# Attention scores: the low half of the rotary queries in 64-row matmuls, two chunks of keys at a time

## The chip, the core and the metric

The kernel runs on one core of a Trainium2 chip. The metric is the device time of one execution in microseconds, and the kernel before is known by the median of three runs. The engines are TensorE (PE; its weight loads have a row of their own, PEld), VectorE (DVE), ScalarE (ACT), GpSimd (POOL) and the DMA queue that SyncE (SP) issues.

## What is computed

One layer of a hybrid block: a projection of 2048 latent tokens and 256 context tokens (width 1024) feeds latent attention with 4 heads and a pooling branch, and both go through one output projection. The change touches the scores of the attention alone:

```python
q = concat([q_nope, rope(q_rope)])          # 4 heads, 128 + 64
k = concat([k_nope, rope(k_rope)])          # rotary keys shared by the heads, scaled per head
s = einsum('bhqd,bhkd->bhqk', qblk, k_all) * (128 + 64) ** -0.5
p = softmax(s)                              # over 256 context keys and 2048 latent keys
o = einsum('bhqk,bhkd->bhqd', p, v_all)
```

## The kernel before

All products are made from halves, since one 16-bit number is not exact enough: each operand is a high f16 number and a low one (the remainder), written by `split()` (L99 and L100: ScalarE copies the high part, VectorE subtracts it). A product is then a sum of three: high by high, high by low, low by high.

In the first 500 us or so the kernel projects the tokens. `tok()` makes the keys of 128 tokens at a time (tile j, 18 in all). The rotary part of a key has only 64 numbers, so its high and its low half lie side by side in `krp` and are transposed together (L554): in the key tile `kd[..., 2, ...]`, partitions 0 to 63 hold the high half and 64 to 127 the low one. The rotary queries are loaded twice, to partitions 0 to 63 and to 64 to 127 (`load_q`). One matmul over 128 rows thus gives q times (high + low).

Attention goes over 16 blocks of 512 queries (4 heads by 4), each in two halves p and two blocks of 128 queries i: `scores(p, i)` is called 64 times, and "a block" below is one such call. It goes over five chunks of keys, CHUNKS, four of 512 and one of 256. For each chunk five matmuls of 128 rows are accumulated in one PSUM bank (L775): three for the 128 plain dimensions, then the high rotary queries by both halves of the keys, then the low rotary queries by both. The banks of the four big chunks come from pool A with 5 buffers, that of the last from pool X. After each chunk VectorE takes the row maximum (L778). After the last come the maximum over the chunks (L783) and its scaling (L784); ScalarE then takes the exponentials of the five banks (L796), which frees the banks, and VectorE transposes them by squares (L799). The DMA queue carries these squares across partitions (`shuffle`, L814).

Some 28 steps of scores behind, `pv()` multiplies with the values: ScalarE and GpSimd (now and then VectorE) split the probabilities (L857, L861), and TensorE runs 54 matmuls of 256 columns for each half p (L824), in a bank of pool O or X. `norm()` transposes row sums of 4 columns on TensorE (L884), and `finish()` makes three more products for each 512 queries (L916). `attn()` interleaves the two by its yields: after each chunk of scores, as many steps of `pv()` as are due. The order of each engine's instructions is then fixed at compile time by a list scheduler that estimates durations.

The startup has small matmuls that the prediction uses: L302 (weights of 2 columns), L308 (a stationary tile of 2 rows), L311 and L330 (128 rows, one moving column), L247 (448 columns).

Of the kernel before, what the change touches and what calls it, by code (L numbers as in the profile page):

```python
# [13 lines left out]
AX = mybir.AxisListType  # L14
# [15 lines left out]
KW = 1536  # L30
# [31 lines left out]
CHUNKS = ((0, 512), (512, 512), (1024, 512), (1536, 512), (2048, 256))  # L62
# [4 lines left out]
def tile_hybrid_block(ctx: ExitStack, tc: tile.TileContext, x, c, cx, c_ctx, w_mod, b_mod, norm_g,  # L67
                      w_in, q_lora_g, w_uq, kv_lora_g, w_ukv, q_norm_g, k_norm_g, w_pool,
                      pool_scale, w_out, rope_t, edge_t, out):
    nc = tc.nc  # L70
# [3 lines left out]
    q_norm_g, k_norm_g, pool_scale, c = q_norm_g[0], k_norm_g[0], pool_scale[0], c[0]  # L74
# [13 lines left out]
    def st(tag, shape, dt=F32):  # L88
        return sb.tile([128] + list(shape), dt, tag=tag, bufs=BUFS[tag], name=nm(tag))

    def pt(tag, shape=(512,), dt=F32):
        return ps.tile([128, *shape], dt, tag=tag, bufs=PBUFS[tag], name=nm("p" + tag))

    def small(n, tag):
        return sm.tile([128, n], F32, tag=tag, name=nm(tag))

    def split(src, hi, lo, eng=None):

        a = nc.scalar.activation(out=hi, in_=src, func=AF.Copy)  # L99
        (eng or nc.vector).tensor_tensor(out=lo, in0=src, in1=hi if hi.dtype == F16 else hi.bitcast(F32),  # L100
                                         op=ALU.subtract)
        return a.ins
# [290 lines left out]
    for i, g in ((0, q_norm_g), (1, k_norm_g)):  # L393
        nc.sync.dma_start(out=gr[:, i, 0], in_=g[DN:].partition_broadcast(128))
        a, b = (gr[:, i, j].rearrange("p (a b c) -> p a b c", a=2, b=2) for j in range(2))
# [43 lines left out]
    def tok(hf, k):  # L439
        is_c = hf == "c"  # L440
        c0 = QR if is_c else 0
        j = k if is_c else 2 + hf * 2 + k
# [3 lines left out]
        p = tokp.pop((hf, k), None)  # L446
        if p is None:
            p = pt("A")
# [52 lines left out]
        krs = st("U", [H, DR])  # L501
        krp = st("U", [H, 2, DR], F16)
        for h in range(H):
# [3 lines left out]
        nc.vector.tensor_tensor(out=kn, in0=k4, in1=rk.unsqueeze(2).broadcast_to([128, H, 128]), op=ALU.mult)  # L507
        nc.vector.tensor_tensor(out=krs, in0=kr.unsqueeze(1).broadcast_to([128, H, DR]),
                                in1=rk.unsqueeze(2).broadcast_to([128, H, DR]), op=ALU.mult)
        split(krs, krp[:, :, 0], krp[:, :, 1])  # L510
        ksl = slice(j * 128, (j + 1) * 128)
        if not is_c:

# [3 lines left out]
            for b in range(2):  # L517
                qp = pt("A")
                n = 0
                for i in range(2):  # L520
                    for a, w in ((lh, 0), (lh, 1), (ll, 0)):
                        nc.tensor.matmul(qp[:, 0:384], lhsT=a[:, i, :], rhs=uq[w][:, i, b * 384:(b + 1) * 384],  # L522
                                         start=(n == 0), stop=(n == 5))
# [10 lines left out]
            for a in range(2):  # L534
                for b in range(2):
                    o = a * 32 + b * 16
# [154 lines left out]
    for key, s0 in zip(TOK_ORDER, TOK_STEPS):  # L691
        g = tok(*key)
        if key in tokp:
            next(g)
        for d in AT:
            plan.setdefault(s0 + d, []).insert(0, g)
# [51 lines left out]
    def flat(t):  # L748
        return t.rearrange("p a b c d -> p (a b c d)")

    def ksegs(c0, w):
        segs = []
        while w:
            i, o = divmod(c0, KW)
            n = min(w, KW - o)
            segs.append((i, o, n))
            c0, w = c0 + n, w - n
        return segs

    def scores(p, i):  # L760

        blk = blocks[p // 2]
        kt, q = K[blk[0]], qop[blk]
        if i == 0:
            if p < 2:
                tbuf.append(st("W", [4, 2, NJ, 32]))
            TP[p] = tbuf[p % 2]
        mx = small(8, "mx")
        sp = []
        for n, (c0, w) in enumerate(CHUNKS):  # L770
            b = pt("A" if n < 4 else "X")
            s0 = 0
            for ki, o, sn in ksegs(c0, w):
                for m, (a, c, kc) in enumerate(((0, 0, 0), (0, 0, 1), (0, 1, 0), (1, 0, 2), (1, 1, 2))):
                    nc.tensor.matmul(b[:, s0:s0 + sn], lhsT=q[:, a, c, p % 2, i], rhs=kt[ki][:, kc, o:o + sn],  # L775
                                     start=(m == 0), stop=(m == 4))
                s0 += sn
            nc.vector.reduce_max(mx[:, n:n + 1], b[:, :w], axis=AX.X)  # L778
            sp.append(b)
            if n < 4:  # L780
                yield
        ng = small(1, "nm")
        nc.vector.reduce_max(ng, mx[:, 0:5], axis=AX.X)  # L783
        nc.vector.tensor_scalar(out=ng, in0=ng, scalar1=nescale, scalar2=PG * LN2, op0=ALU.mult, op1=ALU.add)  # L784
        rs = small(5, f"rs{p % 2}{i}")
        if p == NP - 1:

            for n, (c0, w) in enumerate(CHUNKS):
                nc.scalar.activation(out=flat(TP[p])[:, i * NKEY + c0:i * NKEY + c0 + w], in_=sp[n][:, :w], func=AF.Exp,
                                     bias=ng, scale=escale, accum_out=rs[:, n:n + 1])  # L790
            RS.setdefault(p // 2, []).append(rs)
            yield
            return
        for n, (c0, w) in enumerate(CHUNKS):
            e = st("T", [512])
            nc.scalar.activation(out=e[:, :w], in_=sp[n][:, :w], func=AF.Exp, bias=ng, scale=escale,  # L796
                                 accum_out=rs[:, n:n + 1])
            j0, j1 = c0 // 128, (c0 + w) // 128
            nc.vector.transpose(TP[p][:, :, i, j0:j1, :].rearrange("p q j b -> p j q b"),  # L799
                                e[:, :w].rearrange("p (j q b) -> p j q b", q=4, b=32))  # L800
        RS.setdefault(p // 2, []).append(rs)
        yield
# [192 lines left out]
    def attn():  # L995

        done = 0
        for p in range(NP):
            if p % 2 == 0 and p // 2 + 1 < len(blocks):
                load_q(blocks[p // 2 + 1])  # L1000
            gc = p * PER
            h = p // 8 + 1
            for i in range(2):
                for _ in scores(p, i):
                    gc += 1
                    lag = LAG - max(0, min(LAG - LAG_LAST, (gc - LAG_END * PER) / 4))
                    while done < (gc - lag) * 9 / PER:
                        next(pg)
                        done += 1
                    yield  # L1010
            if p == NP - 1:
                return
            with tc.issue_after(shuffle(p)):
                if h < H and p % 8 in K_PF:
                    load_k(h, (K_PF.index(p % 8),))
                if p in WO_PF:
                    load_wo(*WO_PF[p])
                if p == 30:
                    pairs.append(load_pair(0))
# [216 lines left out]
```

## Time and profile before

| | us |
|---|---|
| median of three runs | 1248.5 (1246.05 to 1248.69) |
| the profiled execution | 1248.26 |
| its span, first to last instruction | 1246.5 |
| score matmuls (L775), first to last start | 513.3 to 1054.7 |

The profile is of one execution. Busy times of TensorE are modelled from the start of a matmul to the end of its tail, so consecutive matmuls overlap in it: the time from one start to the next (the pitch) is what a matmul costs. Matmul lines of the timeline merge runs of equal instructions: the start of the first, the time to the end of the last, and their count. "128\*128 128x512" is a stationary tile of 128 rows and 128 columns, and a moving one of 512 columns.

### The profile page before, as it was taken

The page shows a single profiled execution, that of the slowest core. Times are in us where ns is not written, and L with a number is a line of the kernel's source. Part 1 is how long each engine was busy: PE and PEld are TensorE (multiplying, and loading weights), DVE is VectorE, ACT ScalarE, POOL GpSimd, SP SyncE. Part 2 cuts the span into 40 slices and gives each one's busy share as a digit, 9 for nine tenths or more (in the row PEclk, how much of TensorE's full clock was granted, in tenths as well). Part 3 has the DMA queues.
Part 4 walks back from the last instruction along what each step waited for, and adds up shares of the span by engine and source line. Part 5 has one row for each costly group of instructions (what it writes and reads, how often), then busy time and mean ns, then how long its engine had stood idle before and what let it go on. Part 6 is the DMA issues. An engine that isn't in the chain of part 4 may idle for free.

```text
span 1246.5 us, 22420 instructions
## 1 busy us (share of the span) xinstructions
PE 1186.4 (95%) x7709; PEld 936.6 (75%) x7709; DVE 914.2 (73%) x1706; ACT 761.6 (61%) x1840; POOL 602.7 (48%) x666
## 2 busy tenths in 40 slices
PE   7799999989999999889999999999999999799998
PEld 3598989989899999765666666666666666688886
DVE  4976655666556646469888788878887786999886
ACT  5585655636666655357777777777777777643221
POOL 3745313523435424014655656565565666236666
PEclk9799999999999999999999999999999999999999
DMA  9546851486326746746987797878877798515532
GB/s 304 157 130 143 212 148 45 117 201 195 86 51 149 170 91 157 197 94 151 231 198 193 169 228 192 193 187 196 227 192 191 185 244 208 181 65 206 187 130 98
DMA packets 211272, 208.67 MB, mean 167 GB/s; under 512 B 92452, under 2 KB 168533, under 8 KB 211031
## 3 DMA queue, kind: packets, MB, share of 16 engines
q1 hardware_dynamic: 211158, 207.25, 63.7%
q8 instruction: 60, 0.98, 0.3%
q14 instruction: 54, 0.43, 0.1%
HBM read 98.50 MB, written 35.56 MB: 108 GB/s over the span
## 4 chain that ended last, share of the span: by engine, by line
PE 79%; DMA 7%; ACT 5%; DVE 5%; SPq 2%; issue 2%; POOL 1%; DVEq 0%; ACTq 0%; POOLq 0%
PE pA L775 20%; PE pA L591 18%; PE pA L1049 12%; PE pA L247 6%; PE pO L824 5%; PE pX L824 5%; PE pA L522 3%; PE pX L775 2%; ACT T L796 2%; DMA M<-in_w_in_dram 2%; ACT M L857 2%; SPq L814 2%; PE pA L497 1%; DMA qrd<-U 1%; DMA B<-in_w_mod_dram 1%
## 5 line engine op out<-in xcount | busy, mean ns | idle before, releaser
L861 POOL TENSOR_TENSOR M<-W,M 128x512 f16<-128x512 f32 x244 | 277.5, 1158 | 249.1 <-ACT M L857 219.0
L775 PE MATMUL pA<-B,M 128*128 128x512 f16 x1280 | 299.5, 379 | 17.0 <-ACT T L796 14.1
L591 PE MATMUL pA<-W,B 128*128 128x256 f32 x2304 | 307.4, 287 | 0.1
L591 PEld LDWEIGHTS pA<-W,B 128*128 128x128 f32 x2304 | 290.2, 192 | 3.5 <-issue 0.9
L775 PEld LDWEIGHTS <-M 128*128 128x128 f16 x1600 | 155.6, 98 | 158.8 <-issue 20.1
L799 DVE STREAM_TRANSPOSE W<-T 128x512 f32<-128x512 f32 x310 | 193.2, 641 | 72.9 <-ACT T L796 65.8
L857 ACT ACTIVATE M<-W 128x512 f16<-128x512 f32 x279 | 164.6, 634 | 110.8 <-PE pX L824 42.4
L824 PEld LDWEIGHTS <-B 128*128 128x128 f16 x1728 | 167.7, 98 | 52.7 <-issue 16.6
L796 ACT ACTIVATE T<-pA,nm,gm 128x512 f32<-128x512 f32 x248 | 188.8, 770 | 13.6 <-DVE nm L784 13.5
L778 DVE TENSOR_REDUCE mx<-pA 128x1 f32<-128x512 f32 x256 | 169.3, 672 | 11.2 <-PE pA L775 10.6
L1049 PE MATMUL pA<-W,M 128*128 128x512 f32 (+1 forms) x528 | 120.9, 388 | 2.3 <-DVE M L1055 2.3
L824 PE MATMUL pO<-M,B 128*128 128x256 f16 x864 | 112.8, 273 | 3.8 <-POOL M L861 1.9
L824 PE MATMUL pX<-M,B 128*128 128x256 f16 x864 | 111.1, 273 | 5.3 <-DVE M L861 2.7
L1049 PEld LDWEIGHTS pA<-W,M 128*128 128x128 f32 x528 | 98.6, 190 | 22.8 <-DVE M L1055 2.7
L247 PE MATMUL pA<-B,W 128*128 128x448 f32 (+1 forms) x288 | 85.8, 369 | 0.0
L100 DVE TENSOR_TENSOR B<-M,B 128x1024 fp32r<-128x1024 f32 x48 | 61.6, 1285 | 33.0 <-ACT B L99 32.8
L99 ACT ACTIVATE B<-M 128x1024 fp32r<-128x1024 f32 (+2 forms) x53 | 55.2, 1043 | 45.7 <-DMA M<-in_w_in_dram 38.2
L1041 POOL TENSOR_TENSOR B<-T,B 128x512 f32<-128x512 f32 x31 | 50.2, 1621 | 29.5 <-DVE T L1076 27.6
L1041 POOL TENSOR_TENSOR T<-T,M 128x512 f32<-128x512 f32 x27 | 43.0, 1593 | 38.4 <-DVE T L1090 27.8
L247 PEld LDWEIGHTS pA<-B,W 128*128 128x128 f32 x288 | 54.3, 195 | 4.3 <-DVE T L278 0.9
L247 PE MATMUL pA<-W,W 128*128 128x448 f32 (+1 forms) x144 | 52.7, 367 | 0.0
L1054 ACT ACTIVATE M<-B 128x512 fp32r<-128x512 f32 x32 | 19.7, 628 | 51.6 <-PE pA L1049 39.1
(215 smaller groups left out, 1749.3 us busy)
## 6 DMA issues: line engine op xcount, KB each, us to landing
W<-W SPq DMA_DIRECT2D x496, 144.0 KB
M<-in_w_in_dram SPq DMA_DIRECT2D x48, 512.0 KB
B<-in_x_dram SPq DMA_DIRECT2D x16, 512.0 KB
B<-brd SPq DMA_DIRECT2D x8, 1024.0 KB
B<-in_x_dram SPq DMA_DIRECT2D x8, 1024.0 KB
out_dram<-B SPq DMA_DIRECT2D x31, 256.0 KB
brd<-T SPq DMA_DIRECT2D x24, 256.0 KB
kd<-T SPq DMA_DIRECT2D x36, 128.0 KB
```

The source lines that it names most:

```text
L100: (eng or nc.vector).tensor_tensor(out=lo, in0=src, in1=hi if hi.dtype == F16 else hi.bitcast(F32), op=ALU.subtract)
L247: nc.tensor.matmul(p[:, c0:NTOK], lhsT=a[:, kt, k * 128:(k + 1) * 128], rhs=b, start=(kt == 0 and n == 0), stop=(kt == KT - 1 and n == 2))
L591: nc.tensor.matmul(p[:, i * HB:(i + 1) * HB], lhsT=w[:, a, kt, :], rhs=b[:, kt, :], start=(m == 0), stop=(m == 23))
L775: nc.tensor.matmul(b[:, s0:s0 + sn], lhsT=q[:, a, c, p % 2, i], rhs=kt[ki][:, kc, o:o + sn], start=(m == 0), stop=(m == 4))
L778: nc.vector.reduce_max(mx[:, n:n + 1], b[:, :w], axis=AX.X)
L796: nc.scalar.activation(out=e[:, :w], in_=sp[n][:, :w], func=AF.Exp, bias=ng, scale=escale, accum_out=rs[:, n:n + 1])
L799: nc.vector.transpose(TP[p][:, :, i, j0:j1, :].rearrange("p q j b -> p j q b"), e[:, :w].rearrange("p (j q b) -> p j q b", q=4, b=32))
L824: i = nc.tensor.matmul(o, lhsT=V[0][:, j, a], rhs=t[:, c, jj], start=(j == 0 and m == 0), stop=(j == NJ - 1 and m == 2))
L857: a = nc.scalar.activation(out=t[:, 0], in_=s2, func=AF.Copy)
L861: lo = eng.tensor_tensor(out=t[:, 1], in0=s2, in1=t[:, 0], op=ALU.subtract)
L1041: eng.tensor_tensor(out=o[:, c0:c1] if op == ALU.mult else xr[:, k, n, c0:c1], in0=o[:, c0:c1], in1=a[:, c0:c1], op=op)
L1049: nc.tensor.matmul(b[:, c0:c1], lhsT=c[:, x0, kt, :], rhs=w[x1][:, kt, c0:c1], start=(first and kt == kts[0] and m == 0), stop=(last_ and ...
```

## The change

In `scores()` the first four matmuls of the big chunks stay as they are. The fifth, the low rotary queries, leaves out low by low: it multiplies with the high half of the keys alone, so it has 64 rows. It is put off until two chunks have had their four, and then two such matmuls follow one another, one for each chunk: that of the even chunk on partitions 0 to 63, that of the odd chunk on 64 to 127, each into the bank of its chunk. For this, `tok()` stores the rotary keys of odd chunks the other way round, low above high. The row maxima of two chunks follow the pair. The chunk of 256 keeps its five matmuls of 128 rows.

```diff
-        split(krs, krp[:, :, 0], krp[:, :, 1])
+
+        c = j // 4 % 2
+        split(krs, krp[:, :, c], krp[:, :, 1 - c])
...
-    def ksegs(c0, w):
...
         for n, (c0, w) in enumerate(CHUNKS):
             b = pt("A" if n < 4 else "X")
-            s0 = 0
-            for ki, o, sn in ksegs(c0, w):
-                for m, (a, c, kc) in enumerate(((0, 0, 0), (0, 0, 1), (0, 1, 0), (1, 0, 2), (1, 1, 2))):
-                    nc.tensor.matmul(b[:, s0:s0 + sn], lhsT=q[:, a, c, p % 2, i], rhs=kt[ki][:, kc, o:o + sn],
-                                     start=(m == 0), stop=(m == 4))
-                s0 += sn
-            nc.vector.reduce_max(mx[:, n:n + 1], b[:, :w], axis=AX.X)
             sp.append(b)
+            ki, o = divmod(c0, KW)
+            for m, (a, c, kc) in enumerate(((0, 0, 0), (0, 0, 1), (0, 1, 0), (1, 0, 2), (1, 1, 2))[:5 if n == 4 else 4]):
+                nc.tensor.matmul(b[:, 0:w], lhsT=q[:, a, c, p % 2, i], rhs=kt[ki][:, kc, o:o + w],
+                                 start=(m == 0), stop=(m == 4))
+            if n in (1, 3):
+
+                for d in (0, 1):
+                    ki, o = divmod(CHUNKS[n - 1 + d][0], KW)
+                    r = slice(64 * d, 64 * d + 64)
+                    nc.tensor.matmul(sp[n - 1 + d], lhsT=q[r, 1, 1, p % 2, i], rhs=kt[ki][r, 2, o:o + w],
+                                     start=False, stop=True)
+            for d in {1: (0, 1), 3: (2, 3), 4: (4,)}.get(n, ()):
+                nc.vector.reduce_max(mx[:, d:d + 1], sp[d][:, :CHUNKS[d][1]], axis=AX.X)
             if n < 4:
                 yield
```

## Rows read from the trace of the kernel before

**Rows 1.** The page: engines' busy time, and the chain that ended last.

```profile
PE 1186.4 (95%) x7709; PEld 936.6 (75%) x7709; DVE 914.2 (73%) x1706; ACT 761.6 (61%) x1840; POOL 602.7 (48%) x666
...
PE 79%; DMA 7%; ACT 5%; DVE 5%; SPq 2%; issue 2%; POOL 1%; DVEq 0%; ACTq 0%; POOLq 0%
```

**Rows 2.** Windows: engines' busy time in us, clock, DMA; the startup's row TensorE alone.

```profile
27.86:30.36 2.50, 2.48 (x17) 1.00 1.10 356
...
617.00:681.00 64.00, 62.58 (x413) 40.39 (x411) 52.36 (x113) 47.75 (x112) 39.16 (x34) 1.00 0.80 195
...
sum 320.00, PE 312.92 PEld 201.20 DVE 263.74 ACT 241.28 POOL 189.01; mean PE 62.58 PEld 40.24 DVE 52.75 ACT 48.26 POOL 37.80
```

**Rows 3.** Groups by line, TensorE, 640.81 to 773.45 us: count | busy us, mean ns.

```profile
L775 PE MATMUL pA<-B,M 128*128 128x512 f16 x321 | 75.3, 379 | 2.8 <-ACT T L796 2.8
L824 PE MATMUL pO<-M,B 128*128 128x256 f16 x217 | 28.5, 273 | 0.0
L824 PE MATMUL pX<-M,B 128*128 128x256 f16 x216 | 28.0, 273 | 0.0
L775 PE MATMUL pX<-B,M 128*128 128x256 f16 x80 | 11.3, 273 | 0.0
```

**Rows 4.** Timeline of TensorE in attention: start us, us to the last end, instruction, count.

```profile
807.04 3.40 PE L775 MATMUL pA<-B,M 128*128 128x512 f16 x15
810.28 0.71 PE L775 MATMUL pX<-B,M 128*128 128x256 f16 x5
810.82 0.38 PE L824 MATMUL pX<-M,B 128*128 128x256 f16 x2
811.04 0.27 PE L884 MATMUL pO<-ident,s 128*4 128x128 f32 x1
811.15 1.04 PE L824 MATMUL pX<-M,B 128*128 128x256 f16 x8
```

**Rows 5.** Timeline of TensorE, startup: tiles of 2 and 128 rows by turns.

```profile
28.24 0.38 PE L311 MATMUL pX<-ones,T 128*128 128x1 f32 x2
28.55 0.38 PE L308 MATMUL pX<-ident,T 2*128 2x2 f32 x2
...
30.10 0.38 PE L311 MATMUL pX<-ones,T 128*128 128x1 f32 x2
```

**Rows 6.** Timeline of TensorE, startup: runs of one shape.

```profile
18.61 1.05 PE L308 MATMUL pX<-ident,T 2*128 2x2 f32 x8
...
91.34 0.95 PE L330 MATMUL pX<-ones,M 128*128 128x1 f32 x8
92.15 0.36 PE L591 MATMUL pA<-W,B 128*128 128x256 f32 x1
```

**Rows 7.** Timeline of TensorE, startup: 448-column matmuls, then weights of 2 columns.

```profile
22.93 0.36 PE L247 MATMUL pA<-B,W 128*128 128x448 f32 x1
23.13 0.37 PE L247 MATMUL pA<-W,W 128*128 128x448 f32 x1
23.43 1.02 PE L302 MATMUL pO<-W,sc 128*2 128x512 f32 x2
```

**Rows 8.** Transposes of f16 with 128 columns: timeline, then the group by line.

```profile
97.82 0.40 PE L554 MATMUL pX<-ident,U 128*128 128x128 f16 x4
...
L554 PE MATMUL pX<-ident,U 128*128 128x128 f16 x72 | 7.1, 221 | 0.0
```

**Rows 9.** Timeline of all engines at the end of a block's scores.

```profile
809.26 1.91 DVE L778 TENSOR_REDUCE mx<-pA 128x1 f32<-128x512 f32 x3
...
811.09 0.41 DVE L778 TENSOR_REDUCE mx<-pX 128x1 f32<-128x256 f32 x1
...
811.78 0.21 DVE L784 TENSOR_SCALAR nm<-nm,gm 128x1 f32<-128x1 f32 x1
...
812.37 0.76 ACT L796 ACTIVATE T<-pA,nm,gm 128x512 f32<-128x512 f32 x1
```

**Rows 10.** Waits of TensorE, 600 to 1000 us: total us, times, longest us.

```profile
PE pA L775 <- ACT T L796: 8.0, 18, 0.7
```

More of the change, by code (lines that the diff above doesn't have):

```diff
@@ L749, in flat @@
         return t.rearrange("p a b c d -> p (a b c d)")
-    def ksegs(c0, w):
[L752 to L758, printed above, removed]
     def scores(p, i):
```

## The prediction

> **What bounds the kernel now.** First the engines' shares and the chain of waits [rows 1]: TensorE is busy for 95% of the span and carries 79% of the chain that ended last; no other engine has over 7%. The change touches the scores, so the stage to read is attention. In five stretches of 64 us [rows 2] TensorE is busy for 62.6 of 64 us at granted clock 1.00, its level of 2.4 GHz; VectorE for 52.8, ScalarE for 48.3, GpSimd for 37.8 (means). TensorE is the bound, but a busy figure counts the modelled tails, so I take pitches instead.
>
> The stretch from 640.81 to 773.45 us holds 80 matmuls of 256 columns into pX, five for each call of scores(), so 16 calls ("blocks" of 128 queries) in 132.64 us, 8.29 us each [rows 3]. The pitch of the 512-column score matmuls is (3.40 - 0.379)/14 = 0.216 us, that of the 256-column ones (0.71 - 0.273)/4 = 0.109 us [rows 3, 4]. The count times the pitch gives 320 x 0.216 + (80 + 433) x 0.109 + 12 products of finish at about 0.24 = 69.1 + 55.9 + 2.9 = 127.9 us. So 4.7 us of 132.6, or 0.3 us of a block's 8.29, is not TensorE's issue. Part of it is a wait of the score matmuls for the exponentials that free their PSUM bank: between 600 and 1000 us, 18 times and 8.0 us in all [rows 10]. A TensorE microsecond more or less per block should therefore show almost whole in the time.
>
> **What goes.** In each of 64 blocks, four full 512-column matmuls (low half of the rotary queries) become four of 64 rows, in two pairs. The number of matmuls stays at 25. Each stream is still 512 columns: in this trace a stationary tile of 2 rows has the same pitch as one of 128 rows, (1.05 - 0.25)/7 = 0.114 us against about (92.15 - 91.34)/8 = 0.10 [rows 6], so fewer rows do not shorten a matmul. All of the gain must come from the two of a pair running at the same time, on rows 0 to 63 and 64 to 127 and into two banks. No matmuls of this trace run so, and the bounds are plain: nothing gained, or one pitch of 0.216 us a pair. There are 2 x 64 = 128 pairs, so 0 to 27.6 us. I take the whole pitch, because the pair shares neither stationary rows, moving partitions nor bank, and no row here speaks for a wait between two such matmuls.
>
> **What comes: the change of shape.** This is what decides. The startup alternates two matmuls with a stationary tile of 2 rows (L308) with two of 128 rows (L311), all f32, at granted clock 1.00 [rows 2]. Each group of two starts (30.10 - 28.24)/6 = 0.31 us after the last [rows 5]; two inside a run of one shape take 2 x 0.114 = 0.23 [rows 6]. A change of shape thus costs 0.08 us, and there the load (the bound of these tiny matmuls) is in both figures. It is not the type: L330, f32 with 128 rows, stands between 128-row matmuls of another type and costs nothing extra, its eight and the next start fill 0.81 us [rows 6]. Behind a long stream the same: 448-column matmuls have a pitch of 0.20 us, and the next of another shape (2 columns of weights) starts 0.30 after the last, 0.10 more [rows 7]. One row speaks against it: the transposes of norm(), with 4 columns of weights, stand between 256-column streams at 0.11 us on either side [rows 4], with no loss. But those are narrow in columns, and they are transposes; the 2-row case is the nearest to 64 rows, and I follow it.
>
> The Trainium skill (TensorEngine Tiling (Array Packing), section Tiling Modes) says that a change of tiling mode drains TensorE, while another tile of the same mode does not. Rows 5 agree with it at 0.08 us a change; rows 4 show none at the transposes. It speaks against this change, and it names no duration, so by it the sum stays what the rows make it; without it rival 1 holds. The Trainium skill (TensorE: Matmul & The Clock Gate, Part 3, The mechanism) also says that matmuls on different row groups overlap, starting some 4 ns apart; by that a pair would gain 0.21 us ahead of its changes, an estimate from that page and the pitch. No run here shows the overlap so far.
>
> Each pair stands between full matmuls, so it changes the shape twice: 2 x 0.08 to 0.10 us. Now add the loads. In the stream a load hides behind the matmul ahead (loads are busy for 937 us beside the matmuls, [rows 1]); after a change it stands open. Four f16 matmuls of 128 columns have a pitch of (0.40 - 0.221)/3 = 0.06 us, and that is at least what the load takes [rows 8]. Two open loads (into the pair, and out of it) are 0.12, at the least 0 if a load could slip ahead, and a third, of the pair's second half, is 0 to 0.06.
>
> Sum per pair: changes 0.17 + loads 0.12 (to 0.18) - one matmul saved 0.216 = +0.07 to +0.13, middle 0.10 us. For 128 pairs +9 to +17, middle +13 us.
>
> **What is late next.** The row maxima of chunks 0 and 2 now wait for the pair behind chunks 1 and 3. Those of chunks 0 and 1 are covered by the matmuls of chunks 2 to 4. Those of 2 and 3 both begin after the second pair and stand ahead of chunk 4's, and behind them the negated maximum (L784) and the exponentials, which free the banks. In the block at 809 us three reductions of 0.65 ran in a row anyway, since VectorE had been busy with transposes, and chunk 4's followed, then L784 ended at 811.99 and the exponential began at 812.37 [rows 9]; score products ended at 810.99. After the change two reductions of 0.65, one of 0.41 and 0.45 for the rest end about 2.2 us after the pair, chunk 4's products some 0.55 after it; so the exponentials are at most 0.5 us later. This matters only where a score matmul waits for them, 18 of 48 blocks [rows 10]; it could cost 0 to 24 x 0.5 = 12 us over 64 blocks, but attention's products with the values are at hand to fill, so I take +2. Against that, a slower TensorE eats some of its idle 0.3 us per block (up to 19 us in all); I take -2.
>
> **At nothing:** the swapped halves of the rotary keys (18 token tiles, of which 8 change) are the same two instructions at other columns; the loads of keys move the same bytes. The removed helper never split a chunk: 512 x 3 = 1536 ends a key tile exactly.
>
> **Sum.** 13 + 2 - 2 = +13 us. The profiled execution took 1248.3 us (span 1246.5 and 1.8 around it), 0.2 below the median of 1248.5, so 1261 us either way; its own range is +5 to +22, 1253 to 1270.
>
> **Rivals.**
> 1. *The change of shape is free* (other side). Then each pair saves its 0.216, up to 27.6 us. The transposes of rows 4 speak for it, rows 5 and 7 against. What decides is one figure: if a change with its open load costs under 0.108 us, two cost less than the matmul saved. Not all would arrive, since the score matmuls already wait for exponentials and those come later: 12 to 27 us less, about 20, so 1221 to 1236 us.
> 2. *Shape changes cost, and the two halves do not overlap.* Then nothing is saved: 0.29 to 0.35 x 128 = +37 to +45, about 1289 us. For it: no row shows two matmuls at once.
> 3. *It does nothing*: no overlap and no cost of the change of shape, or the two cancel. Then only late maxima are left, 0 to +6: 1247 to 1254 us.
>
> **How the numbers follow.** Forecast 50%, rival 1 27%, rival 2 10%, rival 3 13%. The predicted time is the likeliest's, 1261. To hold 8 in 10 the range takes all of the forecast and of rival 3 (63) and some two thirds of rival 1 (18): 1226 to 1270. A difference of 0.2% (2.5 us) is about what can be told here. Faster: rival 1 and a little, 28%. Same: half of rival 3 and the lower edge of the forecast, 10%. Slower: the rest, 62%.
>
> **What the profile will show.** Right: the two 64-row matmuls of a pair start within some 0.06 us; the next full load starts 0.08 to 0.1 us after their streams' end; from the last full matmul ahead of a pair to the first behind it some 0.75 us where 0.65 was before; a block takes about 8.5 us in place of 8.29; VectorE's share of attention falls slightly. Wrong: a full-row load or matmul that starts while the pair is in flight (rival 1), starts 0.2 us or more apart inside a pair (rivals 2 and 3), or score matmuls waiting for exponentials in most blocks with sums well over 8 us, which would make the late maxima and not the shape the cause. The work out of attention should keep its times.

## The result, and the profile after

The change makes the kernel slower: 1295.1 us (median of four, 1293.4 to 1295.8) against 1247.8, ratio 1.038 [1.036, 1.040]. The forecast was 1261, and 1226 to 1270 should have held it. It did not.

The page of the kernel after, engines' busy time and the chain that ended last, against [rows 1]:

```profile
PE 1237.4 (96%) x7709; PEld 911.9 (71%) x7709; DVE 924.1 (72%) x1706; ACT 763.2 (59%) x1840; POOL 601.5 (47%) x666
...
PE 80%; DVE 7%; DMA 5%; ACT 4%; issue 2%; SPq 1%; POOL 0%; DVEq 0%; ACTq 0%; POOLq 0%
```

The number of instructions is the same on every engine, and TensorE holds 51 us more while the busy times of VectorE, ScalarE and GpSimd move by 10 us at most. Its waits did not grow either; from 600 to 1000 us the kernel after has one line, where [rows 10] has 8.0 us and 18 times:

```profile
PE pA L768 <- ACT T L795: 7.6, 16, 0.7
```

So the time is in TensorE itself and not in a wait for another engine. The length of a block is read from the exponentials of the last chunk, one for each block: count, then first and last start. The kernel before, 600 to 1000 us:

```profile
L796 ACT ACTIVATE T<-pX,nm,gm x49: 563/568/573, 599.5 to 999.4; 128x256 f32<-128x256 f32 x49
```

The kernel after, same stretch:

```profile
L795 ACT ACTIVATE T<-pX,nm,gm x44: 564/568/572, 601.4 to 995.4; 128x256 f32<-128x256 f32 x44
```

(999.4 - 599.5)/48 = 8.33 us a block before, (995.4 - 601.4)/43 = 9.16 after: 0.83 us more, which would be 53 us over 64 blocks. From the first score matmul to the last it is 588.8 us (512.1 to 1100.9) against 541.6 (513.3 to 1054.9; the 1054.7 of the table is the last weight load): 47 us, all of the change, so the first and last blocks lose less than these. The rest of the kernel kept its time. The timeline of TensorE shows where the 0.83 lies (kernel after, one block; full score matmuls are L768, those of 64 rows L775, products with the values L823; compare [rows 4]):

```profile
819.76 0.38 PE L768 MATMUL pA<-B,M 128*128 128x512 f16 x1
820.07 0.39 PE L775 MATMUL pA<-B,M 64*128 64x512 f16 x1
820.39 0.61 PE L823 MATMUL pX<-M,B 128*128 128x256 f16 x4
820.84 1.03 PE L768 MATMUL pA<-B,M 128*128 128x512 f16 x4
821.79 0.39 PE L775 MATMUL pA<-B,M 64*128 64x512 f16 x1
822.11 1.04 PE L768 MATMUL pA<-B,M 128*128 128x512 f16 x4
823.08 0.39 PE L775 MATMUL pA<-B,M 64*128 64x512 f16 x1
823.40 1.04 PE L768 MATMUL pA<-B,M 128*128 128x512 f16 x4
824.38 0.39 PE L775 MATMUL pA<-B,M 64*128 64x512 f16 x1
824.70 0.72 PE L768 MATMUL pX<-B,M 128*128 128x256 f16 x5
```

There are no pairs here. The source puts the two 64-row matmuls behind the full ones of two chunks; on the engine the first of them stands right behind its own chunk's four, and the full ones of the next chunk come in between. So the scheduler that fixes the order at compile time drew it ahead. Why it did is a reading that no run tested: the operands of the first are there as soon as its own chunk's four are issued, whereas the next chunk may have to wait for a bank. Of the 256 matmuls of 64 rows, 250 stand alone in the trace; three pairs stand together, and their two start 3 ns apart.

Each lone one changes the shape twice. The last of the four full ones starts at 820.84 + 1.03 - 0.379 = 821.49, the 64-row one at 821.79, 0.30 later, and the next full one 0.32 after that, where the pitch was 0.216. From the unrounded starts of the whole trace the two steps are 0.312 us (median of 252) and 0.320 (of 253). That is 0.20 us for each lone one, and 256 x 0.20 = 51 us. The weight loads show the same from the other side (after, TensorE's loads; the last brackets are idle time ahead of them):

```profile
821.79 0.09 PEld L775 LDWEIGHTS <-M 64*128 64x128 f16 x1 [0.42 <-issue]
822.11 0.55 PEld L768 LDWEIGHTS <-M 128*128 128x128 f16 x4 [0.23 <-issue]
```

In a stream of one shape a load starts some 2 ns after the start of the matmul ahead (median of 528, 600 to 1000 us), and so hides behind it. A load of the other shape starts 0.31 us after that start, past the pitch of 0.216, and its own matmul 4 ns later. How much of the 0.10 us is the load and how much the change, these records cannot tell. The view of L775 shows that it is so each time: the load engine sat idle ahead of its loads 252 times, 106.8 us in all, and no semaphore is behind it. This is not the time lost, since most of each 0.42 us lies under the matmul ahead.

```profile
L775 PEld LDWEIGHTS <-M x256: 92/93/94, 517.5 to 1100.9; 64*128 64x128 f16 x128
...
  issue: 106.8, 252
```

### The profile page after: what moved, and what is told of

Read it like the earlier page. It is cut to its first block, busy times and chain, and to the rows that moved or that the text cites. A ratio compares the mean times of both kernels' runs of the same rounds, so it can differ in the third digit from the quotient of the medians.

```text
span 1291.6 us, 22420 instructions
## 1 busy us (share of the span) xinstructions
PE 1237.4 (96%) x7709; PEld 911.9 (71%) x7709; DVE 924.1 (72%) x1706; ACT 763.2 (59%) x1840; POOL 601.5 (47%) x666
## 4 chain that ended last, share of the span: by engine, by line
PE 80%; DVE 7%; DMA 5%; ACT 4%; issue 2%; SPq 1%; POOL 0%; DVEq 0%; ACTq 0%; POOLq 0%
PE pA L768 18%; PE pA L593 17%; PE pA L1048 10%; PE pO L823 6%; PE pA L775 6%; PE pA L247 6%; PE pX L823 5%; PE pX L768 3%; PE pA L524 2%; DMA M<-in_w_in_dram 2%; ACT M L856 2%; ACT T L795 1%; DVE W L943 1%; PE pA L497 1%; DVE T L278 1%
## 5 line engine op out<-in xcount | busy, mean ns | idle before, releaser
L768 PE MATMUL pA<-B,M 128*128 128x512 f16 x1024 | 265.4, 382 | 12.9 <-ACT T L795 9.6
L778 DVE TENSOR_REDUCE mx<-pA 128x1 f32<-128x512 f32 x256 | 173.5, 679 | 48.3 <-PE pA L775 47.7
L768 PEld LDWEIGHTS <-M 128*128 128x128 f16 x1344 | 117.9, 98 | 123.4 <-issue 51.9
L823 PEld LDWEIGHTS <-B 128*128 128x128 f16 x1728 | 161.7, 98 | 48.7 <-issue 30.6
L823 PE MATMUL pX<-M,B 128*128 128x256 f16 x864 | 111.4, 273 | 5.3 <-DVE M L860 2.7
L823 PE MATMUL pO<-M,B 128*128 128x256 f16 x864 | 112.9, 273 | 2.0 <-POOL M L860 1.1
L775 PEld LDWEIGHTS <-M 64*128 64x128 f16 x256 | 23.5, 93 | 106.9 <-issue 106.8
L775 PE MATMUL pA<-B,M 64*128 64x512 f16 x256 | 98.0, 387 | 0.0
```

The source lines that it names most:

```text
L768: nc.tensor.matmul(b[:, 0:w], lhsT=q[:, a, c, p % 2, i], rhs=kt[ki][:, kc, o:o + w], start=(m == 0), stop=(m == 4))
L775: nc.tensor.matmul(sp[n - 1 + d], lhsT=q[r, 1, 1, p % 2, i], rhs=kt[ki][r, 2, o:o + w], start=False, stop=True)
L778: nc.vector.reduce_max(mx[:, d:d + 1], sp[d][:, :CHUNKS[d][1]], axis=AX.X)
L823: i = nc.tensor.matmul(o, lhsT=V[0][:, j, a], rhs=t[:, c, jj], start=(j == 0 and m == 0), stop=(j == NJ - 1 and m == 2))
```

## Experiments

Theory A: the two of a pair were drawn apart; each 64-row matmul pays two changes of shape and overlaps nothing. Theory B: the later row maxima make the loss. Theory C: the two halves of the array do not work at the same time. The kernels of the experiments write a block with helpers: `full(n, terms)` issues full matmuls of chunk n (T4: the first four, T5: all five), `rows64(n, d, after)` the 64-row one of chunk n on half d and orders it behind the instruction `after`, `maxima(...)` the row maxima. They were built from the kernel after, e10 from the kernel before; the cuts of e2 and e3 are shown against e1. Where a time lies outside what was expected of it, the text says so.

**e1, the pair held together.**

```diff
-                    nc.tensor.matmul(sp[n - 1 + d], lhsT=q[r, 1, 1, p % 2, i], ...)
+                    last = rows64(n - 1 + d, d, last)   # behind the last full one of the odd chunk
```

> The pair is held together by an order: the first 64-row matmul may not stand ahead of the last full one of the odd chunk. Theory A (the compile-time scheduler drew the two of a pair apart, so that each 64-row matmul paid its own two changes of shape and overlapped with nothing): the two start 3 ns apart, a pair adds 0.10 + 0.10 and saves 0.216 us, 128 x -0.016 = -2 us, so 1246 us (1240 to 1254). Theory B (the late row maxima make the loss): still 1285 or more. Theory C (the two halves of the array do not overlap): 128 x 0.20 = +26 us, 1273.

Measured: 1259.6 us, ratio 1.007 [1.005, 1.009], somewhat over the 1254 that theory A allowed. TensorE's timeline of e1 (full L767, 64 rows L775):

```profile
792.88 1.02 PE L767 MATMUL pA<-B,M 128*128 128x512 f16 x4 [0.81 <-ACT T L810]
793.83 0.39 PE L775 MATMUL pA<-B,M 64*128 64x512 f16 x2
794.16 0.83 PE L838 MATMUL pO<-M,B 128*128 128x256 f16 x6
```

The two matmuls start 3 ns apart (all 128 pairs), and the next one starts 0.33 us after them, the step that a lone one takes. So they run at the same time, and theory C falls. Some 38 of the 47 us are back by the order alone, so theory B is not the main cause. The block takes what it took before:

```profile
L810 ACT ACTIVATE T<-pX,nm,gm x48: 563/568/573, 603.2 to 995.0; 128x256 f32<-128x256 f32 x48
```

(995.0 - 603.2)/47 = 8.34. The 8 us that e1 lacks to the kernel before are not in these blocks; more on that with e5.

**e2, full matmuls in the pair's place.**

```diff
-                    last = rows64(n - 1 + d, d, last)
+                    x = full(n - 1 + d, T5[4:], start=False, stop=True)   # 128 rows, ordered behind last
```

> The postponed fifth matmuls of two chunks have 128 rows, as before the change; they stand where e1 has its pair and the maxima come as late. Theory A: no change of shape is left, so as the kernel before or a little over, 1248 to 1254 us. Theory B: the maxima are as late as in the change, so about 1290. Theory C: as A.

Measured: 1261.8 us, ratio 1.009 [1.007, 1.012], between the two theories. Putting off the fifth matmuls and the maxima costs something, yet not in the steady part, where a block takes (997.9 - 605.9)/47 = 8.34 us:

```profile
L812 ACT ACTIVATE T<-pX,nm,gm x48: 563/568/573, 605.9 to 997.9; 128x256 f32<-128x256 f32 x48
```

With e1 this prices the pair: two changes of shape against one matmul saved, and no difference.

**e3, both on one half.**

```diff
-                    last = rows64(n - 1 + d, d, last)
+                    last = rows64(n - 1 + d, 0, last)   # keys not swapped
```

> As e1, but both 64-row matmuls of a pair stand on partitions 0 to 63 and the keys of odd chunks are not swapped. Theory A: the streams follow one another, two changes a pair and nothing saved, 128 x 0.20 = +26 us, 1273. Theory B: as e1, 1285 or more. Theory C: no difference to e1.

Measured: 1281.3 us, ratio 1.025 [1.023, 1.028]; theory A had 1273, and the 8 us over it are what e1 lacks too. The timeline of e3 (64 rows L774), and its blocks:

```profile
805.81 1.02 PE L766 MATMUL pA<-B,M 128*128 128x512 f16 x4 [0.81 <-ACT T L809]
806.76 0.60 PE L774 MATMUL pA<-B,M 64*128 64x512 f16 x2
807.30 0.83 PE L837 MATMUL pO<-M,B 128*128 128x256 f16 x6
```

```profile
L809 ACT ACTIVATE T<-pX,nm,gm x46: 563/568/573, 606.4 to 999.6; 128x256 f32<-128x256 f32 x46
```

Here the two take 0.60 us, one stream behind the other; a block takes (999.6 - 606.4)/45 = 8.74. Against e2 that is 0.40 us for two pairs that save nothing: four changes of shape at 0.10 us each, the open load included. Against e1 it is 0.40 for two matmuls of overlap.

**e9, lone ones without postponing.**

```diff
             last = full(n, T5 if n == 4 else T4, stop=n == 4)
+            if n < 4:
+                rows64(n, n % 2, last)
+            maxima(n)
```

> Each 64-row matmul stands alone in the place of the old fifth one (right behind the four of its chunk), and the row maximum follows at once, as before the change: only the shape is changed, nothing is postponed. Theory A (256 lone 64-row matmuls at two changes of 0.10 us each): 51 us more, 1299 (1293 to 1302), as slow as the change or slower. Rival (a part of the change's 47 us comes from the postponed maxima): 1290 or less.

Measured: 1295.8 us, ratio 1.039 [1.038, 1.041], and blocks of (997.0 - 602.9)/43 = 9.17 us, as in the change:

```profile
L809 ACT ACTIVATE T<-pX,nm,gm x44: 562/569/576, 602.9 to 997.0; 128x256 f32<-128x256 f32 x44
```

What the change did on the chip is this: four lone 64-row matmuls a block, 8 x 0.10 us. Nothing need be postponed for it. Theory A stands.

**e4, all four in one group.**

```diff
+            if n < 3:
+                last = full(n, T4)
+            elif n == 3:
+                for m in (3, 2, 1, 0):          # that of chunk 3 opens its bank
+                    last = rows64(m, m % 2, last, start=m == 3, stop=m < 3)
+                maxima(0, 1, 2)
+                full(3, T4, start=False, stop=True)
+                maxima(3)
```

> All four 64-row matmuls of a block stand in one group: after the full ones of chunks 0 to 2, that of chunk 3 opens its bank, then 2, 1 and 0; the full ones of chunk 3 follow. Two changes of shape a block and two matmuls saved. Theory A: 64 x (0.20 - 0.432) = -15 us, 1233 (1229 to 1240). Theory B: 1270 or more. Theory C: 64 x 0.20 = +13, 1261.

Measured: 1255.4 us, ratio 1.005 [1.003, 1.006], outside all three ranges. The matmuls did what theory A says (timeline of e4): four in 0.61 us, and the next starts 0.54 after the group.

```profile
804.82 1.03 PE L767 MATMUL pA<-B,M 128*128 128x512 f16 x4
805.78 0.61 PE L775 MATMUL pA<-B,M 64*128 64x512 f16 x4
806.32 1.90 PE L767 MATMUL pA<-B,M 128*128 128x512 f16 x8
```

But the gain of 15 us did not come: its blocks from 600 to 1000 us take (998.4 - 606.0)/47 = 8.35 us. Waits of TensorE in e4, 560 to 1040 us (total us, times, longest):

```profile
PE pX L844 <- DVE M L881: 11.1, 7, 1.6
PE pA L767 <- ACT T L816: 6.8, 13, 1.4
```

and the largest for VectorE's half in the kernel before, same stretch:

```profile
PE pO L824 <- DVE M L861: 0.9, 1, 0.9
```

The products with the values now wait for a half of the probabilities that VectorE makes (j2 = 4, one in nine) and that stands behind a burst of maxima; e7 tests this.

**e8 and e11, how much there is to gain.** e8 has four full matmuls for the big chunks and no low rotary queries; e11 is e8 with the half j2 = 4 on GpSimd.

```diff
+            full(n, T4, stop=True)
+            maxima(n)
```

> The product of the low rotary queries is left out for the four big chunks (four full matmuls each and nothing else): the most that any form of the pair could bring. If TensorE alone set the pace: 64 x -0.864 = -55 us, 1193. If other waits take over soon, as theory E has it: -10 to -30, 1218 to 1238.

> As e8 (the product of the low rotary queries left out for the four big chunks), with the half j2 = 4 on GpSimd. Theory E (in e8 TensorE waits mostly for VectorE's halves, 17 us of waits): 1212 to 1222. Rival (GpSimd's halves or the exponentials hold it just as well): 1228 or more.

Measured: e8 1230.1 us, ratio 0.985 [0.984, 0.987]; e11 1225.1, ratio 0.982 [0.980, 0.984]. So with the whole product gone, 0.864 us of TensorE a block, 18 us of 55 arrive. e11 lies between its two ranges. TensorE's waits in e8, 560 to 1010 us, and its blocks from the ninth to the 57th, the same 48 as in the line of the kernel before, (981.0 - 600.0)/48 = 7.94 us:

```profile
PE pX L835 <- DVE M L872: 12.4, 12, 1.6
PE pX L835 <- POOL M L872: 9.7, 28, 0.7
PE pO L835 <- POOL M L872: 6.1, 16, 0.9
PE pO L835 <- DVE M L872: 4.8, 7, 1.3
```

```profile
L807 ACT ACTIVATE T<-pX,nm,gm x49: 564/567/572, 600.0 to 981.0; 128x256 f32<-128x256 f32 x49
```

TensorE leads the stage by only about 0.39 us a block; behind that stand the halves, from VectorE and from GpSimd. Without work on the halves, a form of the pair could hardly bring more than these 18 us. With VectorE's half moved, e11's same blocks take 7.76 us, 0.18 less, of which a part is lost again in its last blocks.

**e5, e6, e7: the old form in the first 4 and last 8 blocks.**

```diff
-        (the block of e1, or of e4)
+        yield from (grouped() if 2 <= p < 28 else plain())     # e5: e1's block, e6 and e7: e4's
...
-            eng = nc.vector if j2 == 4 or (p == NP - 2 and j2 % 2) else nc.gpsimd
+            eng = nc.vector if p == NP - 2 and (j2 % 2 or j2 == 4) else nc.gpsimd     # e7 alone
```

> As e1 in the 52 blocks from the fifth to the 56th; the first 4 and the last 8 have five full matmuls and the maxima at once, as before the change. Theory D (in the steady part e1 costs what the kernel before costs, 8.32 us a block against 8.34; its loss lies in the first and last blocks, where TensorE is not the bound and the later maxima and longer held banks count): 52 x -0.016 = -1 us, so 1246 to 1250. Rival (the late maxima cost in every block): as e1, 8 to 10 over the kernel before.

> As e4 (one group of four, two changes of shape a block) in the same 52 blocks, the first 4 and last 8 as before the change. Theory D with the matmul time of the group: 52 x -0.23 = -12, 1236. Theory E (a faster TensorE now waits for the halves of the probabilities, of which VectorE makes one in nine behind a burst of maxima; in the steady part of e4 a block took 8.38 us): 52 x +0.04 = +2, 1248 to 1252.

> As e6, and the one half in nine that VectorE makes (j2 = 4) goes to GpSimd, which was busy for 30 of 50 us there. Theory E: the waits for VectorE's halves go, and most of the 0.23 us a block arrives, 1236 to 1242. Rival (GpSimd, at 1.16 us a half, or the exponentials set the pace instead): 1248 or more.

Measured: e5 1253.1 us, ratio 1.004 [1.003, 1.006]; e6 1253.1, 1.004 [1.003, 1.006]; e7 1243.5, 0.997 [0.996, 0.998]. e5 lies between its two ranges, and e6 and e7 lie one to two us above the nearer of theirs. e5 got back the first blocks: the fifth block's last exponential starts at 569.2 us; 571.4 in the kernel before, 573.3 in e1. Over all traces with the old form in the first four blocks (before, e5, e6, e7, e10, e12) it starts at 566.2 to 572.3, and with the fifth matmuls put off and held together (e1 to e4) at 573.3 to 576.2. So there the late maxima and the banks held longer do cost, but how much cannot be told from one trace each.

e5 did not get back the last blocks, though they are plain again: from the 58th block to the 62nd it takes 43.0 us (1006.9 to 1049.9) against 36.8 (1008.4 to 1045.2). What differs there is the order of the queues. The DMA queue in e5:

```profile
1021.39 0.61 SPq L913 DMA_DIRECT2D rvd<-rr  x1
1022.04 0.27 SPq L915 DMA_DIRECT2D rvd<-rr  x1
1027.16 0.34 SPq L918 DMA_DIRECT2D T<-rvd  x1
1031.11 2.27 SPq L840 DMA_DIRECT2D W<-W  x2
```

and in the kernel before:

```profile
1009.40 0.26 SPq L889 DMA_DIRECT2D rvd<-rr  x1
1010.08 10.69 SPq L814 DMA_DIRECT2D W<-W  x16
...
1021.59 0.78 SPq L892 DMA_DIRECT2D T<-rvd  x1
...
1027.32 1.78 SPq L814 DMA_DIRECT2D W<-W  x3
```

Before, the 16 transfers of a shuffle stand between the row sums' way out and their way back, which hides the 5 us of that trip; in e5 the load back stands right behind and holds the queue until 1027.16. The next shuffle begins at 1031.1 in place of 1027.3. All fourteen traces divide by this order. Where the shuffle stands between (before, after, e4, e8, e9), the stretch from the 58th block to the 62nd takes 36.0 to 38.8 us; where it does not (e1, e2, e3, e5, e6, e7, e10, e11, e12), 40.8 to 44.7. e4, with 36.0, has it as the kernel before:

```profile
1017.35 0.34 SPq L909 DMA_DIRECT2D rvd<-rr  x1
1018.03 12.54 SPq L834 DMA_DIRECT2D W<-W  x16
...
1031.39 0.74 SPq L912 DMA_DIRECT2D T<-rvd  x1
```

So the order and the late blocks go together, in kernels of every form. That the order is the cause is still argued; no run set it by hand.

e7 shows e4's group at work once VectorE's half is out of the way: blocks of (991.9 - 606.1)/47 = 8.21 us, where e6 has (995.6 - 604.6)/47 = 8.32 and the kernel before 8.33.

```profile
L828 ACT ACTIVATE T<-pX,nm,gm x48: 563/568/573, 606.1 to 991.9; 128x256 f32<-128x256 f32 x48
```

**e10, control of e7:** the kernel before with the half moved, and nothing else.

> Control of e7: the kernel before with only the half j2 = 4 moved from VectorE to GpSimd, five full matmuls everywhere. If e7's gain is the group's with VectorE's wait out of the way, this one brings little by itself, 1245 to 1249 us. If the moved half is the gain, it is as fast as e7, 1243 to 1244.

Measured: 1253.0 us, ratio 1.005 [1.003, 1.006], above both ranges. A part of this lies in the last blocks, which are late here too (41.1 us). But its blocks in between are slower as well, (1000.1 - 596.6)/48 = 8.41 us:

```profile
L796 ACT ACTIVATE T<-pX,nm,gm x49: 563/568/572, 596.6 to 1000.1; 128x256 f32<-128x256 f32 x49
```

The moved half alone brings nothing there, so the gain of e7 is the group's, with the half as its condition.

**e12, the half moved in the middle only.**

```diff
+            eng = nc.vector if j2 == 4 and not 2 <= p < 26 or (p == NP - 2 and j2 % 2) else nc.gpsimd
```

> As e7, but the half j2 = 4 goes to GpSimd only for the query halves p from 2 to 25, and stays with VectorE in the first two and the last six. If the last blocks of e7 are slow because of the moved half (41.6 us from the 58th block's exponentials to the 62nd's, against 36.8 before), 4 us less than e7: 1238 to 1241. If they are slow because of the order in which the DMA queue and TensorE got their work (e5 has 43.0 there with no half moved), as e7: 1242 to 1245.

Measured: 1247.4 us, ratio 0.9995 [0.998, 1.001]; a miss for both. The last blocks stay slow, 41.1 us (1004.4 to 1045.5) against e7's 41.6, so the moved half is not their cause; the blocks of the middle are e7's (8.20), and the loss to e7 is in the first ones (the fifth block's last exponential at 572.3 against 568.9). The half on VectorE does not explain that: e6 has it there too, and reaches the same point at 566.2. What moves the first blocks by these few us stays open.

## Why the prediction was wrong

**What bounds.** Right for added work: 0.83 us of TensorE a block arrived whole. Wrong as "more or less": of work taken away only 0.39 of 0.86 us arrives (e8). The idle 0.3 us a block were read as slack of TensorE alone; the halves behind it were not looked at.

**The step that failed** is "each pair stands between full matmuls, so it changes the shape twice", with "I take the whole pitch" for the overlap. Both took the order of the source for the order of the engine. The front of this document says that a scheduler fixes it; the prediction never asked what it would do with a matmul that may be ready before the next chunk's. On the chip a pair was two lone matmuls, four changes and nothing saved: 0.83/2 = 0.41 us a pair where +0.10 was forecast. One of its own signs of being wrong did come, starts more than 0.2 us apart inside a pair (820.07 and 821.79), but it was put down to rivals 2 and 3. None of the rivals named this cause. Rival 2 comes near in time (1289) by another mechanism, and e1 refutes that one: the halves do overlap.

**The price of a change of shape** was right in kind and somewhat high. Forecast: 0.08 to 0.10 and an open load of 0.06, so 0.15; measured 0.10 with the load in it (e3 against e2). The startup's two-row matmuls of [rows 5] were the right rows to read, and the transposes of [rows 4] the wrong ones for 64 rows. The Trainium skill's drain at a change of tiling mode (TensorEngine Tiling (Array Packing), Tiling Modes) agrees with the runs, with 0.10 us beside it. So an adjacent pair is worth 0.216 - 0.20, next to nothing: for such a pair what decides is, as rival 1 had it, whether a change costs more or less than 0.108 us, and it is almost exactly that. Even with its pairs adjacent, then, the forecast's +13 us would have been too much for the steady blocks, where e1 costs nothing. The +8 us of e1 lie in the forecast's range only by luck: they come from the first and last blocks.

**What is late next.** +2 us was taken for late maxima. In the steady blocks they cost nothing (e2 8.34, before 8.33); in the first and last blocks e2 loses 11 us, near the upper bound of 12 but in another place than was said, and e5 shows that the part in the last blocks is not the maxima's. The -2 us, idle time that a slower TensorE would eat, did not come: its waits stayed at 7.6 us where they were 8.0, and a block grew by 0.83 us for 4 x 0.20 us of changes.

**Open:** what tips the compile-time order of the DMA queue in the last blocks, and whether it alone makes them late. They take 4 to 8 us more than before in e1, e2, e3, e5, e6, e7, e10, e11 and e12, and not in e4.

## What to carry to other kernels

A row-tiled matmul pays by what stands next to it: read the compiled order of TensorE, or the timeline, before the overlap is counted, and tie the partners together where a scheduler may draw them apart. Two changes of shape cost as much as one 512-column matmul saves, so a single pair breaks even and a group of four gains one matmul on TensorE, 0.23 us a block, of which 0.12 arrived in e7. Before work is taken off an engine, leave all of it out in one run: that shows which wait is next, and how little the best form could bring.

## What the runs showed of the hardware

Two f16 matmuls of 64 rows on the two halves of the array run at the same time: a pair takes 0.39 us against 0.60 on one half (e1, e3), a group of four 0.61 (e4). Between shapes of 64 and 128 rows TensorE loses 0.10 us each way (steps of 0.312 and 0.320 us in place of 0.216); the load of the new shape starts 0.31 us after the start of the last matmul of the old one, and not beside it. The forecast had the load on top of that; it is within it.
